# Rotary rows of two heads' queries and keys gathered into one 128-partition tile, turned there in four passes, and brought back

## The chip, the cores and the metric

The kernel runs on one core of a Trainium2 chip. The core has a matrix engine (TensorE, PE in the profile; PEld is its weight load), a vector engine (VectorE, DVE), a scalar engine (ScalarE, ACT), a general engine (GpSimd, POOL) and a synchronisation engine (SyncE, SP). Each takes its instructions in order from its own queue. Transfers are carried by 16 DMA engines and are issued here from SP, ACT and POOL. SBUF is the working memory with 128 partitions, PSUM holds the matmul accumulators, DRAM holds inputs, outputs and scratch. The metric is the device time of one execution in microseconds.

## The reference

A model of two layers for one sequence of 512 tokens of width 1024: an attention layer with three dilations, an mLSTM layer, and a gated feed-forward layer after each. Weights and activations are float32. The change lies in the attention layer, which for each of three groups projects queries, keys and values for eight heads of width 128, turns the first 32 of the 128 features of each query and key by the token's position, and attends within a window:

```python
def apply_partial_rope(t, positions):            # ROT_DIM = 32
    half = ROT_DIM // 2
    inv_freq = ROPE_THETA ** (-jnp.arange(half) * 2.0 / ROT_DIM)
    ang = positions[..., None] * inv_freq
    x1, x2 = t[..., :half], t[..., half:ROT_DIM]
    return concatenate([x1 * cos - x2 * sin, x2 * cos + x1 * sin, t[..., ROT_DIM:]])

def dilated_attention_mixer(xn, positions, w_in, w_out):
    proj = (xn @ w_in).reshape(B, S, N_GROUPS, 3, ATTN_HEADS, ATTN_HEAD_DIM)
    for g, (window, dilation) in enumerate(((128, 1), (512, 4), (2048, 16))):
        q = apply_partial_rope(proj[:, :, g, 0], positions) * scale
        k = apply_partial_rope(proj[:, :, g, 1], positions)
        o, lse = dilated_window_attention(q, k, proj[:, :, g, 2], window, dilation)
        ...
    wts = softmax(stack(lses))          # over the three groups
    return (sum over g of wts * o) @ w_out
```

## The kernel before

Activations lie with features on partitions and the 512 tokens along the free side. Every float32 product is made of three matmuls in a reduced float32 format, from high and low parts of weights and activations: ScalarE makes the high part of a weight chunk (line 208) and VectorE the low part (line 209), from a 512 KB load issued by SP (line 200). Three buffers each hold raw, high and low chunks, so the parts of a chunk are made about two chunks before TensorE uses them.

The attention layer works through four pairs of heads (`attention_pair`). For a pair it projects, for each of the groups 0, 1 and 2, the queries and then the keys of both heads (`project`, two chunks of 24 matmuls each, two accumulators of 128 features by 512 tokens). Then come the values of group 0 (two chunks) and the values of groups 1 and 2 together (`project_tokens_wide`, four chunks). The profile's names begin with the pair: a1g0q is the query projection of group 0 in pair 1.

An accumulator is left through `evac`: VectorE multiplies it by `rbc`, the inverse root mean square of each token, into a 128x2x512 tile (lines 730 and 732; group 0 changes the order of the tokens on the way). The first 32 partitions of the tile are the rotary rows. Before the change they are turned in three steps: `rope_part` shuffles the accumulator's 32 rows so that each row's partner is in its place (line 535), `rotate` multiplies both heads' shuffled rows by a table of scaled sines (line 538) and adds them (lines 541 and 543). The cosines are already in rows 0 to 31 of `rbc`, put there by `rope_scale` (lines 529 and 530) with the scaling of the token. All these instructions use 32 partitions.

What follows a projection is issued in *runs*, deferred by a counter of *ticks*: `advance` adds a tick after each chunk of a projection and calls what has come due. A run keeps its matmuls together in TensorE's order, and the matmuls of later projections stand behind it (`run`, `fenced`). So on TensorE the place of a run is fixed by its tick. On the other engines the order is set by the framework, by when it expects inputs to be ready. The lists below give the ticks:

```python
RUN_AT = (2, 3, 5, 10)
LAST_AT = (2, 4)
```

The first entry counts from the end of group 0's keys, the other three from the end of group 2's keys. They are:

- `scores0`, the scores of group 0 (matmuls at line 575), their maxima and exponentials;
- `scores12`, the scores of groups 1 and 2 (line 595), likewise;
- one run with `joint` (an exchange of maxima and sums between partitions, matmul at line 631, and the groups' weights), and for each head `weigh`, `transposes` (VectorE at line 687, then four writes to scratch in DRAM from POOL, line 690) and `bring` (one read of 960 KB from scratch, POOL, line 695, into a tile named pT);
- `values`, for each head the product of values and probabilities (lines 705 and 710), which reads pT.

In the last pair `LAST_AT` takes the place of the middle two, and the values are placed by hand among the chunks of the output projection.

POOL also carries, in each pair, the turn of group 0's values through scratch (eight writes of 64 KB at line 675, one read at line 677). Before the loops it copies the tables of sines and cosines into their place (lines 388 and 389).

Of the kernel before, what the change touches and what calls it, by code (L numbers as in the profile page):

```python
# [11 lines left out]
F32 = mybir.dt.float32  # L12
F32R = mybir.dt.float32r
I32 = mybir.dt.int32
AF = mybir.ActivationFunctionType
ALU = mybir.AluOpType
AX = mybir.AxisListType
P = 128

SEQ = 512  # L20
# [11 lines left out]
C1 = 6.28125  # L32
C2 = float(np.float32(np.uint32(np.float32(TWO_PI - C1).view(np.uint32) & 0xFFFFF000).view(np.float32)))
C3 = float(np.float32(TWO_PI - C1 - C2))
RUN_AT = (2, 3, 5, 10)
LAST_AT = (2, 4)
STACK_AT = (9, 11, 15, 17)
HEAD_AT = ((9, 10, 12, 14), (10, 11, 13, 15), (12, 13, 15, 17), (13, 14, 16, 18), (15, 16, 18, 19), (16, 17, 19, 21),
           (18, 19, 21, 22), (19, 20, 21, 23))
# [31 lines left out]
def tile_hybrid_dilated_attn_mlstm(  # L71
# [4 lines left out]
    nc = tc.nc  # L76
    x = x[0]
# [61 lines left out]
    def defer(n, fn):  # L139
        later.append((tick[0] + n, next(order), fn))  # L140
# [166 lines left out]
    def inverse_rms(v, name, box=None, then=None):  # L307

        r = npl.tile([P, TB], F32, tag="rtok", name=name + "r", bufs=2)
        rbc = npl.tile([P, SEQ], F32, tag="rbc", name=name + "rbc")  # L310
        parts = {}

        def finish():
            nc.vector.tensor_scalar(v, v, 1.0 / D, EPS, op0=ALU.mult, op1=ALU.add)
            rsqrt_newton(npl, v, TB, name + "r", r)
            rhl = npl.tile([P, 2, TB], F32R, tag="rhl", name=name + "rhl", bufs=2)
            nc.vector.tensor_copy(rhl[:, 0], r)
            nc.vector.tensor_tensor(rhl[:, 1], r, rhl[:, 0].bitcast(F32), op=ALU.subtract)
            for part in range(2):
                dg = parts[part] = npl.tile([P, SEQ], F32R, tag=("ssum", "sq")[part], name=name + "dg",  # L320
                                               bufs=1 + part)
                for tb in range(TB):
                    nc.vector.tensor_scalar(dg[:, tb * P:(tb + 1) * P], ident,
                                            rhl[:, part, tb:tb + 1].bitcast(F32), None, op0=ALU.mult)

        def hook():
            bp = ps.tile([P, 512], F32, tag="t", name=name + "bc", bufs=1)
            for part in range(2):
                nc.tensor.matmul(bp, ones_r, parts[part], start=(part == 0), stop=(part == 1))
            nc.vector.tensor_copy(rbc, bp)  # L330
            if then is not None:
                then(bp)
        if box is None:
            finish()
        else:
            box["finish"] = finish
        return rbc, r, hook
# [7 lines left out]
    with ExitStack() as actx:  # L345
        ap = pool(actx, "attn")
        dp = pool(actx, "scratch", space=bass.MemoryType.DRAM)

        R = 32
# [1 line left out]
        acst = ap.tile([P, K_END - K_MA], F32, name="acst")  # L351
        part = lambda at, w: acst[:, at - K_MA:at - K_MA + w]
        mask_band, mask_causal, mask_dil, perm = part(K_MA, 2 * P), part(K_M1, P), part(K_M2, P), part(K_G, P)
        cosn, sinn = (ap.tile([R, SEQ], F32, tag="pt", name=nm, bufs=2) for nm in ("cosn", "sinn"))
        sinr = ap.tile([R, SEQ], F32, name="sinr")

        posi = ap.tile([P, SEQ], I32, tag="rt", name="posi", bufs=2)
        nc.scalar.dma_start(posi.rearrange("(c r) s -> c r s", c=4)[:, 0], positions[0:1].to_broadcast([4, SEQ]))
        warm = cp.tile([P, 1], F32, name="warm")
        nc.scalar.activation(warm, ones[:, 0:1], AF.Sin)  # L360
# [19 lines left out]
        def rope_tables():  # L380
            nc.scalar.activation(sn, ang, AF.Sin)
            nc.scalar.activation(cs, ang, AF.Sin, scale=0.5)
            nc.vector.tensor_scalar(sn, sn, cst[:, K_SGN:K_SGN + 1], None, op0=ALU.mult)
            nc.vector.scalar_tensor_tensor(cs, cs, -2.0, cs, op0=ALU.mult, op1=ALU.mult)
            nc.vector.tensor_scalar(cs, cs, 1.0, None, op0=ALU.add)
            for c in range(4):
                s = slice(32 * c, 32 * c + 32)
                nc.gpsimd.tensor_copy(sinn[:, c * P:(c + 1) * P], sn[s])
                nc.gpsimd.tensor_copy(cosn[:, c * P:(c + 1) * P], cs[s])

        def tok_tile(name):
            return ap.tile([P, 2, SEQ], F32, tag="qk", name=name, bufs=6)
# [103 lines left out]
        nc.vector.tensor_tensor(v, ss2[:, 0], ss2[:, 1], op=ALU.add)  # L496
        behind(first_mm, 3)
        box = {}
        rbc, rtok, bc_hook = inverse_rms(v, "x", box, then=lambda bp: rope_scale(bp))
        behind(box["finish"], engine=DVE)  # L500
        both(lambda: ready.append(split_chunk(weight_chunk(w_in, 0, 3 * D, 4, "a0g1q_k0"))))
        for k in range(4, 8):
# [13 lines left out]
        defer(4, natural_rstd)  # L516
        defer(5, transpose_rows)

        def by_block(t):

            return t.rearrange("p (c b j) -> p b c j", c=4, b=TB)

        def in_order(t):
            return t.rearrange("p (b c j) -> p b c j", c=4, b=TB)

        def rope_scale(bp):
            nc.vector.tensor_tensor(sinr, bp[:R], sinn, op=ALU.mult)
            nc.vector.tensor_tensor(rbc[:R], bp[:R], cosn, op=ALU.mult)  # L530

        shift = [(k + 16) % 32 for k in range(32)]

        def rope_part(sh, m, acc):
            nc.vector.stream_shuffle(sh[:, m, :], acc[:R], shift)

        def rotate(t, sh, blocks):
            nc.vector.tensor_tensor(sh, sh, sinr.unsqueeze(1).to_broadcast([R, 2, SEQ]), op=ALU.mult)
            if blocks:
                for i in range(2):  # L540
                    nc.vector.tensor_tensor(in_order(t[:R, i]), in_order(t[:R, i]), by_block(sh[:, i]), op=ALU.add)
            else:
                nc.vector.tensor_tensor(t[:R], t[:R], sh, op=ALU.add)

        o_all = []

# [5 lines left out]
        def attention_pair(pr):  # L552
            nm = "a%d" % pr
# [165 lines left out]
            for g in range(3):  # L719
                base = g * 3 * D + pr * 256  # L720
                qk = []
                qks.append(qk)
                for part in range(2):
                    t = tok_tile("%sg%d_%s" % (nm, g, "qk"[part]))

                    sh = ap.tile([R, 2, SEQ], F32, tag="rt", name="rot", bufs=2)

                    def evac(m, acc, t=t, sh=sh, g=g):
                        if g == 0:
                            nc.vector.tensor_tensor(in_order(t[:, m]), by_block(acc), by_block(rbc), op=ALU.mult)  # L730
                        else:
                            nc.vector.tensor_tensor(t[:, m], acc, rbc, op=ALU.mult)
                        rope_part(sh, m, acc)
                    start = pr == 0 and g == 0 and part == 0
                    if start:
                        def first_evac(evac=evac):
                            bc_hook()
                            for m in range(2):
                                evac(m, facc[m])
                        defer(1, first_evac)  # L740
                    else:
                        project(pair, w_in, base + part * D, KC, evac, "%sg%d%s" % (nm, g, "qk"[part]), ready=ready)
                        if pr == 0 and g == 0:
                            rotate(qk[0], sh0, True)
                    if pr == 0 and g == 0 and part == 0:
                        sh0 = sh
                    else:
                        rotate(t, sh, g == 0)
                    qk.append(t)
                if g == 0:  # L750
                    defer(RUN_AT[0], lambda: run(lambda: scores0(*qks[0])))
            later_runs = (
# [376 lines left out]
    with ExitStack() as mctx:  # L1129
# [136 lines left out]
        i = 0  # L1266
# [275 lines left out]
```

## Time and profile before

| What | us |
|---|---|
| median of three runs | 1428.96 (1428.83 to 1429.31) |
| profiled execution | 1428.88 |
| its span | 1427.1 |
| TensorE busy in the span | 1415.9 |
| VectorE busy | 960.4 |
| ScalarE busy | 603.4 |
| POOL busy | 84.8 |

The attention layer takes about the first third of the span. A line of the timeline gives the start and the length in microseconds, the engine, the line of the kernel, the operation, what it writes and reads, the tile's shape and how many instructions are merged; in square brackets stand the idle time before it and what ended it. A matmul's length is modelled and overlaps the next one's, so the distance of two starts tells more than the length. A DMA line gives the bytes of one issue and the time from issue to landing. For a group of instructions three numbers with slashes are shortest, median and longest, in ns.

### The profile page before, as it was taken

How to read it: one execution, taken by the hardware profiler on the slowest of the kernel's cores; microseconds unless marked ns; L12 is line 12 of the kernel's file. 1: busy time of each engine (PE TensorE's matmuls, PEld its weight loads, DVE VectorE, ACT ScalarE, POOL GpSimd, SP SyncE). 2: the span in 40 equal slices, each digit the busy share in tenths (PEclk: the TensorE clock that was granted, in tenths of full speed). 3: DMA queues.
4: the chain of work that ended last, by engine and by line, in shares of the span. 5: the costliest groups of instructions: out<-in, count | busy, mean ns of one | idle time of the engine just before them, and what ended most of it. 6: DMA issues, size and time to landing. Idle time of an engine off the chain costs nothing. (4 is left out here: it accounts for less than half of the span.)

```text
span 1427.1 us, 20255 instructions
## 1 busy us (share of the span) xinstructions
PE 1415.9 (99%) x7986; PEld 1241.2 (87%) x7986; DVE 960.4 (67%) x1679; ACT 603.4 (42%) x1009; POOL 84.8 (6%) x137
## 2 busy tenths in 40 slices
PE   9999999999999999999999999999999999999998
PEld 7888888888888888999998888888888899998887
DVE  7857567567567397787782358897758777888233
ACT  5333224224225353444462233696534354445123
POOL 1011011011002000000000010110000000001001
PEclk9999999999999999999999999999999999999999
DMA  6346236235335434323233232321133332346331
GB/s 193 102 115 201 75 104 191 97 108 151 133 104 145 145 101 133 107 72 118 90 96 96 96 98 74 104 60 60 55 113 96 122 118 83 96 118 180 116 106 72
DMA packets 133688, 158.67 MB, mean 111 GB/s; under 512 B 7060, under 2 KB 121044, under 8 KB 133592
## 3 DMA queue, kind: packets, MB, share of 16 engines
q1 hardware_dynamic: 125616, 131.55, 29.6%
q0 software_dynamic: 6320, 24.69, 6.2%
q8 instruction: 63, 1.03, 0.3%
q10 hardware_dynamic: 1656, 1.12, 0.2%
q14 instruction: 33, 0.27, 0.1%
HBM read 143.18 MB, written 14.16 MB: 110 GB/s over the span
## 5 line engine op out<-in xcount | busy, mean ns | idle before, releaser
L1471 PE MATMUL fin<-fw_l,f1hh 128*128 128x512 f32 (+1 forms) x198 | 72.5, 366 | 0.0
L1471 PE MATMUL fin<-fw_h,f1hh 128*128 128x512 f32 (+1 forms) x198 | 72.4, 366 | 0.0
L1471 PE MATMUL fin<-fw_h,f1hl 128*128 128x512 f32 (+1 forms) x198 | 72.4, 365 | 0.0
L209 DVE TENSOR_TENSOR fo_k_l<-fo_k_w,fo_k_h 128x1024 fp32r<-128x1024 f32 (+1 forms) x24 | 27.2, 1135 | 62.0 <-ACT fo_k_h L208 62.0
L239 PE MATMUL fo<-f0hh,fo_k_h 128*128 128x512 f32 x176 | 68.5, 389 | 0.0
L239 PE MATMUL fo<-f0hl,fo_k_h 128*128 128x512 f32 x176 | 68.5, 389 | 0.0
L239 PE MATMUL fo<-f0hh,fo_k_l 128*128 128x512 f32 x176 | 68.5, 389 | 0.0
L209 DVE TENSOR_TENSOR fw_l<-fw_w,fw_h 128x1024 fp32r<-128x1024 f32 x22 | 27.1, 1233 | 59.9 <-ACT fw_h L208 59.9
L208 ACT ACTIVATE fo_k_h<-fo_k_w 128x1024 fp32r<-128x1024 f32 (+1 forms) x24 | 23.7, 989 | 74.7 <-PE fo L239 74.7
L208 ACT ACTIVATE fw_h<-fw_w 128x1024 fp32r<-128x1024 f32 x22 | 23.3, 1060 | 67.6 <-PE fin L1471 67.0
L1471 PEld LDWEIGHTS fin<-fw_l,f1hh 128*128 128x128 f32 x198 | 37.4, 189 | 6.2 <-DVE fw_l L209 0.2
L1471 PEld LDWEIGHTS fin<-fw_h,f1hh 128*128 128x128 f32 x198 | 37.3, 189 | 6.2
L1471 PEld LDWEIGHTS fin<-fw_h,f1hl 128*128 128x128 f32 x198 | 37.3, 188 | 6.0
L239 PEld LDWEIGHTS fo<-f0hh,fo_k_l 128*128 128x128 f32 x176 | 33.0, 188 | 6.9
L239 PEld LDWEIGHTS fo<-f0hl,fo_k_h 128*128 128x128 f32 x176 | 33.0, 188 | 6.9
L239 PEld LDWEIGHTS fo<-f0hh,fo_k_h 128*128 128x128 f32 x176 | 33.0, 188 | 6.7
L239 PE MATMUL f0j<-n_h,f0j_h 128*128 128x512 f32 x96 | 37.5, 390 | 0.0
L239 PE MATMUL f1j<-n_h,f1j_h 128*128 128x512 f32 x96 | 37.5, 390 | 0.0
L239 PE MATMUL f0j<-n_h,f0j_l 128*128 128x512 f32 x96 | 37.4, 389 | 0.0
L239 PE MATMUL f1j<-n_h,f1j_l 128*128 128x512 f32 x96 | 37.4, 389 | 0.0
L239 PE MATMUL f0j<-n_l,f0j_h 128*128 128x512 f32 x96 | 37.3, 389 | 0.0
L239 PE MATMUL f1j<-n_l,f1j_h 128*128 128x512 f32 x96 | 37.3, 389 | 0.0
(2105 smaller groups left out, 4886.0 us busy)
## 6 DMA issues: line engine op xcount, KB each, us to landing
f0j_w<-in_ffn_w_in_dram SPq DMA_DIRECT2D x28, 512.0 KB, 4.9
f1j_w<-in_ffn_w_in_dram SPq DMA_DIRECT2D x28, 512.0 KB, 4.4
fw_w<-in_ffn_w_out_dram SPq DMA_DIRECT2D x22, 512.0 KB, 3.9
fo_k_w<-in_ffn_w_out_dram SPq DMA_DIRECT2D x20, 512.0 KB, 3.5
awo_k_w<-in_attn_w_out_dram SPq DMA_DIRECT2D x8, 512.0 KB, 7.1
mv_k_w<-in_mlstm_w_in_dram SPq DMA_DIRECT2D x8, 512.0 KB, 3.7
mqk_k_w<-in_mlstm_w_in_dram SPq DMA_DIRECT2D x8, 512.0 KB, 3.9
mo_k_w<-in_mlstm_w_in_dram SPq DMA_DIRECT2D x8, 512.0 KB, 3.7
```

The lines of the kernel that those rows point to most:

```text
L208: nc.scalar.activation(hi[:, :n], raw[:, :n], AF.Copy)
L209: nc.vector.tensor_tensor(lo[:, :n], raw[:, :n], hi[:, :n].bitcast(F32), op=ALU.subtract)
L239: nc.tensor.matmul(acc, whl[a][:, k, m * P:(m + 1) * P], pairs[b][kk], start=(kk == 0 and (a, b) == SPLITS[0]), stop=(kk == nk - 1 and (a, ...
L1471: nc.tensor.matmul(acc[i][:, cs], a[a_][kk][:, tb * P:(tb + 1) * P], whl[b_][:, k, cs], start=(kk == 0 and (a_, b_) == SPLITS[0]), stop=(k ...
```

## The change

The rotary rows of a group, which are the first 32 partitions of both heads of the query tile and of the key tile, are gathered by four DMAs from POOL (`rope_gather`, `rope_rows`) into a tile `rt` of 128 partitions and 512 tokens. One tick after the keys of the group, `rotate` shuffles `rt` into a second tile, multiplies that by the sines and `rt` by the cosines, adds the two, and brings the four strips of 32 rows back by four more DMAs from POOL. The tables `cos4` and `sin4` are held four times over, on 128 partitions; six DMAs from POOL copy the first 32 rows to the others at the start. The tokens' scale now reaches the rotary rows through `evac` as it does the other rows, so the hook that scaled the tables is gone. The tiles of this work take four buffers of 2 KB a partition instead of two of 4 KB. The runs' ticks become (3, 4, 6, 10) and (3, 5).

```diff
--- before.py
+++ after.py
@@ -32,8 +32,8 @@
 C1 = 6.28125
 C2 = float(np.float32(np.uint32(np.float32(TWO_PI - C1).view(np.uint32) & 0xFFFFF000).view(np.float32)))
 C3 = float(np.float32(TWO_PI - C1 - C2))
-RUN_AT = (2, 3, 5, 10)
-LAST_AT = (2, 4)
+RUN_AT = (3, 4, 6, 10)
+LAST_AT = (3, 5)
 STACK_AT = (9, 11, 15, 17)
 HEAD_AT = ((9, 10, 12, 14), (10, 11, 13, 15), (12, 13, 15, 17), (13, 14, 16, 18), (15, 16, 18, 19), (16, 17, 19, 21),
            (18, 19, 21, 22), (19, 20, 21, 23))
@@ -351,10 +351,9 @@
         acst = ap.tile([P, K_END - K_MA], F32, name="acst")
         part = lambda at, w: acst[:, at - K_MA:at - K_MA + w]
         mask_band, mask_causal, mask_dil, perm = part(K_MA, 2 * P), part(K_M1, P), part(K_M2, P), part(K_G, P)
-        cosn, sinn = (ap.tile([R, SEQ], F32, tag="pt", name=nm, bufs=2) for nm in ("cosn", "sinn"))
-        sinr = ap.tile([R, SEQ], F32, name="sinr")
-
-        posi = ap.tile([P, SEQ], I32, tag="rt", name="posi", bufs=2)
+        cos4, sin4 = (ap.tile([P, SEQ], F32, name=nm) for nm in ("cos4", "sin4"))
+
+        posi = ap.tile([P, SEQ], I32, tag="rt", name="posi", bufs=4)
         nc.scalar.dma_start(posi.rearrange("(c r) s -> c r s", c=4)[:, 0], positions[0:1].to_broadcast([4, SEQ]))
         warm = cp.tile([P, 1], F32, name="warm")
         nc.scalar.activation(warm, ones[:, 0:1], AF.Sin)
@@ -385,8 +384,12 @@
             nc.vector.tensor_scalar(cs, cs, 1.0, None, op0=ALU.add)
             for c in range(4):
                 s = slice(32 * c, 32 * c + 32)
-                nc.gpsimd.tensor_copy(sinn[:, c * P:(c + 1) * P], sn[s])
-                nc.gpsimd.tensor_copy(cosn[:, c * P:(c + 1) * P], cs[s])
+                nc.gpsimd.tensor_copy(sin4[:R, c * P:(c + 1) * P], sn[s])
+                nc.gpsimd.tensor_copy(cos4[:R, c * P:(c + 1) * P], cs[s])
+
+            for t in (sin4, cos4):
+                for c in range(1, 4):
+                    nc.gpsimd.dma_start(t[32 * c:32 * c + 32], t[:R])
 
         def tok_tile(name):
             return ap.tile([P, 2, SEQ], F32, tag="qk", name=name, bufs=6)
@@ -496,7 +499,7 @@
         nc.vector.tensor_tensor(v, ss2[:, 0], ss2[:, 1], op=ALU.add)
         behind(first_mm, 3)
         box = {}
-        rbc, rtok, bc_hook = inverse_rms(v, "x", box, then=lambda bp: rope_scale(bp))
+        rbc, rtok, bc_hook = inverse_rms(v, "x", box)
         behind(box["finish"], engine=DVE)
         both(lambda: ready.append(split_chunk(weight_chunk(w_in, 0, 3 * D, 4, "a0g1q_k0"))))
         for k in range(4, 8):
@@ -516,8 +519,6 @@
         defer(4, natural_rstd)
         defer(5, transpose_rows)
 
-
-
         def by_block(t):
 
             return t.rearrange("p (c b j) -> p b c j", c=4, b=TB)
@@ -525,22 +526,30 @@
         def in_order(t):
             return t.rearrange("p (b c j) -> p b c j", c=4, b=TB)
 
-        def rope_scale(bp):
-            nc.vector.tensor_tensor(sinr, bp[:R], sinn, op=ALU.mult)
-            nc.vector.tensor_tensor(rbc[:R], bp[:R], cosn, op=ALU.mult)
-
         shift = [(k + 16) % 32 for k in range(32)]
 
-        def rope_part(sh, m, acc):
-            nc.vector.stream_shuffle(sh[:, m, :], acc[:R], shift)
-
-        def rotate(t, sh, blocks):
-            nc.vector.tensor_tensor(sh, sh, sinr.unsqueeze(1).to_broadcast([R, 2, SEQ]), op=ALU.mult)
-            if blocks:
-                for i in range(2):
-                    nc.vector.tensor_tensor(in_order(t[:R, i]), in_order(t[:R, i]), by_block(sh[:, i]), op=ALU.add)
-            else:
-                nc.vector.tensor_tensor(t[:R], t[:R], sh, op=ALU.add)
+        def rope_rows(rt, part, m):
+            i = 2 * part + m
+            return rt[R * i:R * (i + 1)]
+
+        def rope_gather(rt, t, part):
+
+            for m in range(2):
+                nc.gpsimd.dma_start(rope_rows(rt, part, m), t[:R, m])
+
+        def rotate(rt, qk, blocks):
+
+            sh = ap.tile([P, SEQ], F32, tag="rt", name="rot", bufs=4)
+            nc.vector.stream_shuffle(sh, rt, shift)
+            for x, table in ((sh, sin4), (rt, cos4)):
+                if blocks:
+                    nc.vector.tensor_tensor(in_order(x), in_order(x), by_block(table), op=ALU.mult)
+                else:
+                    nc.vector.tensor_tensor(x, x, table, op=ALU.mult)
+            nc.vector.tensor_tensor(rt, rt, sh, op=ALU.add)
+            for part, t in enumerate(qk):
+                for m in range(2):
+                    nc.gpsimd.dma_start(t[:R, m], rope_rows(rt, part, m))
 
         o_all = []
 
@@ -720,33 +729,27 @@
                 base = g * 3 * D + pr * 256
                 qk = []
                 qks.append(qk)
+                rt = ap.tile([P, SEQ], F32, tag="rt", name="%sg%drt" % (nm, g), bufs=4)
                 for part in range(2):
                     t = tok_tile("%sg%d_%s" % (nm, g, "qk"[part]))
 
-                    sh = ap.tile([R, 2, SEQ], F32, tag="rt", name="rot", bufs=2)
-
-                    def evac(m, acc, t=t, sh=sh, g=g):
+                    def evac(m, acc, t=t, g=g):
                         if g == 0:
                             nc.vector.tensor_tensor(in_order(t[:, m]), by_block(acc), by_block(rbc), op=ALU.mult)
                         else:
                             nc.vector.tensor_tensor(t[:, m], acc, rbc, op=ALU.mult)
-                        rope_part(sh, m, acc)
-                    start = pr == 0 and g == 0 and part == 0
-                    if start:
-                        def first_evac(evac=evac):
+                    if pr == 0 and g == 0 and part == 0:
+                        def first_evac(evac=evac, rt=rt, t=t):
                             bc_hook()
                             for m in range(2):
                                 evac(m, facc[m])
+                            rope_gather(rt, t, 0)
                         defer(1, first_evac)
                     else:
                         project(pair, w_in, base + part * D, KC, evac, "%sg%d%s" % (nm, g, "qk"[part]), ready=ready)
-                        if pr == 0 and g == 0:
-                            rotate(qk[0], sh0, True)
-                    if pr == 0 and g == 0 and part == 0:
-                        sh0 = sh
-                    else:
-                        rotate(t, sh, g == 0)
+                        rope_gather(rt, t, part)
                     qk.append(t)
+                defer(1, lambda rt=rt, qk=qk, g=g: rotate(rt, qk, g == 0))
                 if g == 0:
                     defer(RUN_AT[0], lambda: run(lambda: scores0(*qks[0])))
             later_runs = (
```

## The prediction

> **What bounds the kernel now.** I read the page first: the span, the engine shares and the chain that ended last; then the time by stretches of the attention stage, then TensorE's own waits.
>
> ```profile
> span 1427.1 us, 20255 instructions
> PE 1415.9 (99%) x7986; PEld 1241.2 (87%) x7986; DVE 960.4 (67%) x1679; ACT 603.4 (42%) x1009; POOL 84.8 (6%) x137
> ...
> PE 34%; DVE 3%; ACT 2%; issue 0%; ACTq 0%; DVEq 0%
> ...
> 0.00:50.00 50.00, 47.61 (x215) 38.27 (x216) 41.14 (x110) 24.27 (x44) 5.79 (x18) 1.00 0.50 158
> ...
> 100.00:150.00 50.00, 50.00 (x263) 42.89 (x262) 33.64 (x93) 19.28 (x50) 6.28 (x11) 1.00 0.56 174
> ...
> 450.00:500.00 50.00, 50.00 (x252) 42.50 (x251) 24.39 (x33) 16.05 (x23) 5.50 (x10) 1.00 0.51 158
> ...
> PE m1yT L305 <- ACT vaug L1169: 1.7, 1, 1.7
> PE idle L107 <- DVE idle_w L102: 1.5, 1, 1.5
> PE a0g0q L449 <- ACT first_h L439: 0.5, 1, 0.5
> PE m1nb L1312 <- ACT m0e L1322: 0.4, 1, 0.4
> PE xbc L329 <- DVE xdg L323: 0.3, 1, 0.3
> ```
>
> In the stretches the columns are length, PE, PEld, DVE, ACT and POOL busy, TensorE's granted clock, DMA share and GB/s. TensorE bounds the stage: it is busy throughout from 50 to 500 us, at full clock, and its waits for other engines come to 4.4 us in the whole program, none of them on the rotary work. VectorE, whose work the change removes, is busy 34 of 50 us. So what it saves buys time only where TensorE waits for it; what it delays costs time where a buffer now comes just in time. I looked for that second kind next: where work of the runs reaches TensorE.
>
> ```profile
> 98.43 3.73 PE L595 MATMUL a0s<-a0g_k,a0g_q 128*128 128x128 f32 x32
> ...
> 112.92 0.38 PE L631 MATMUL a0xps<-a0ex,acst 128*128 128x128 f32 x2
> ...
> 140.39 1.73 PE L705 MATMUL a0o<-a0pT,a0v 128*128 128x128 f32 x14
> ...
> 143.74 1.73 PE L705 MATMUL a0o<-a0pT,a0v 128*128 128x128 f32 x14
> ...
> 255.32 1.73 PE L705 MATMUL a1o<-a1pT,a1v 128*128 128x128 f32 x14
> ...
> 366.90 1.73 PE L705 MATMUL a2o<-a2pT,a2v 128*128 128x128 f32 x14
> ...
> 478.53 1.73 PE L705 MATMUL a3o<-a3pT,a3v 128*128 128x128 f32 x14
> 13.22 1.26 POOL L389 COPY cosn<-angles 32x128 f32<-32x128 f32 x4
> ...
> 128.97 0.56 POOL L695 DMA_DIRECT2D a0pT<-a0pD  x1
> 136.38 0.55 POOL L695 DMA_DIRECT2D a0pT<-a0pD  x1 [6.86 <-DMA a0pD<-a0pB]
> ...
> 247.35 0.55 POOL L695 DMA_DIRECT2D a1pT<-a1pD  x1 [6.36 <-DMA a1pD<-a1pB]
> ...
> 359.23 0.55 POOL L695 DMA_DIRECT2D a2pT<-a2pD  x1 [6.66 <-DMA a2pD<-a2pB]
> ...
> 465.73 0.55 POOL L695 DMA_DIRECT2D a3pT<-a3pD  x1 [6.58 <-DMA a3pD<-a3pB]
> a0pT<-a0pD POOLq DMA_DIRECT2D x1, 960.0 KB, 9.3
> a0pT<-a0pD POOLq DMA_DIRECT2D x1, 960.0 KB, 6.7
> ...
> a1pT<-a1pD POOLq DMA_DIRECT2D x1, 960.0 KB, 5.6
> ...
> a2pT<-a2pD POOLq DMA_DIRECT2D x1, 960.0 KB, 6.9
> ...
> a3pT<-a3pD POOLq DMA_DIRECT2D x1, 960.0 KB, 8.8
> ```
>
> These are TensorE's timeline, POOL's timeline and the DMA view in the window of one issue (last number: us from issue to landing). In pair 0 the second head's probabilities are brought by the issue at 136.38 and land 6.7 later, at 143.08; their first matmul starts at 143.74. The margin is **0.66 us**. In pair 1: 247.35 + 5.6 = 252.95 against 255.32, margin 2.37. Pair 2: 359.23 + 6.9 = 366.13 against 366.90, margin 0.77. Pair 3: 465.73 + 8.8 = 474.53 against 478.53, margin 4.00. The first head's read in pair 0, 128.97 + 9.3 = 138.27 against 140.39, has 2.1. TensorE does not wait here today, but only just.
>
> **The change, part by part.**
>
> *A tick.* The deferred runs are counted in ticks, one for each chunk of a projection; a chunk is 24 matmuls. From the scores (98.43) to the exchange (112.92) lie two ticks and the scores' own run. Taking 3.6 for that run (its 3.73 less the overlap of its last matmul), a tick is (14.49 - 3.6) / 2 = **5.44 us**.
>
> *RUN_AT's third value, 5 to 6, its fourth kept at 10.* The run that holds the exchange, the weighing, the transpositions, the writes to scratch and the reads back moves one tick later. The run of the values stays on its tick. The chain between the two thus loses 5.44 us of room, and it had 0.66, 2.37 and 0.77 us to spare. The exchange's input isn't the limit: the scores move by the same tick. LAST_AT's second value, 4 to 5, does the same to pair 3, which had 4.00.
>
> *Does the chain itself get shorter?* This is VectorE in pair 0:
>
> ```profile
> 113.33 0.29 DVE L633 TENSOR_TENSOR a0ex<-a0xps,cst 128x128 f32<-128x128 f32 x1 [2.84 <-PE a0xps L631]
> ...
> 123.08 1.22 DVE L209 TENSOR_TENSOR a1g0k_k_l<-a1g0k_k_w,a1g0k_k_h 128x1024 fp32r<-128x1024 f32 x1
> 124.21 2.17 DVE L687 STREAM_TRANSPOSE a0pB<-a0p 128x1920 f32<-128x1920 f32 x1
> ...
> 127.41 0.68 DVE L730 TENSOR_TENSOR a1g_q<-a1g0q,xrbc 128x512 f32<-128x512 f32 x1
> L538 DVE TENSOR_TENSOR rot<-rot,sinr x24: 1197/1206/1208, 39.1 to 419.4; 32x1024 f32<-32x1024 f32 x24
> ...
> L535 DVE STREAM_SHUFFLE rot<-a1g0q x2: 719/722/724, 128.0 to 130.3; 32x512 f32<-32x512 f32 x2
> ```
>
> From 113.33 to the end of the second transposition, 126.38, there is no rotary instruction, so nothing that the change removes shortens the chain. Moved to 118.8 to 131.8, it meets the evacuations of the next pair's first block: 127.41, and a second from the same projection. Two at 0.61 of pace (0.68 less overlap) are 1.2 us. Its bounds are 0 (the transposition goes first) and 2.4 (one more weight split of 1.2, as the one at 123.08, falls in). I take 1.2 for pairs 0 to 2, since both evacuations come due inside the moved window, and 0 for pair 3, which has no next pair. The writes and reads by DMA keep their times of today; their bounds are the fastest and slowest row of the read, 5.6 and 9.3.
>
> *The rotation.* Removed in each of 12 group-and-pair blocks: four shuffles of 32x512 (L535, 0.72), two products of 32x1024 (L538, 1.21), and as much again in additions, which I price like the products. A pass over 512 elements takes 0.68 on 128 partitions (L730) and 0.72 on 32 (L535), so its price follows its length and not its partitions; I price each 128x512 pass at 0.7. A block goes from 4 x 0.7 + 4 x 1.2 = 7.6 us to 4 x 0.7 = 2.8, and VectorE loses some 58 us of 960. By the first fence this buys TensorE nothing: 0.
>
> *The gathers and returns.* Each block issues eight 64 KB transfers from POOL, 96 in all, and six more replicate the tables. No row has a copy from SBUF to SBUF; nearest is the 64 KB piece of the value turn, and the slowest read sets the other end:
>
> ```profile
> a0vD<-a0vB POOLq DMA_DIRECT2D x8, 64.0 KB, 3.0
> ...
> L675 POOL DMA_DIRECT2D a0vD<-a0vB x8: 648/648/692, 92.2 to 98.1; - x8
> 128.00:140.39 12.39, 12.39 (x56) 10.25 (x55) 8.16 (x14) 2.15 (x3) 1.97 (x4) 1.00 0.99 339
> ```
>
> Per block the new path is: two issues (1.3), landing (3.0), four passes (2.8), four issues (2.6), landing (3.0): 12.7 us after the last evacuation. For the scores of group 0 the run now stands three ticks after the block, 16.3 us, plus the values of two heads, 2 x 3.35 (143.74 - 140.39), in pairs 1 to 3; for groups 1 and 2 it stands four ticks after group 2, 21.8 us, and three, 16.3, in pair 3. Covered by 3.6 us in pair 0 and at pair 3's end and by 9 or more elsewhere: 0. If that cover goes, TensorE stands at the scores. With both landings at 9.3 the path is 25.3 us: 9.0 late in pair 0, 2.3 late three times for group 0, 3.5 late three times for groups 1 and 2, and 9.0 late at pair 3's end. That is the upper end, 36 us. I take 0, the row of equal size being the nearest; the other is of fifteen times the bytes.
>
> VectorE waits in order for the gather. Behind it queue weight splits, made two chunks (10.9 us) ahead, and the next evacuation of an accumulator (room about 5 us); a wait of 4.3 us (1.3 + 3.0) fits. POOL's queue: in pairs 0 to 2 the gathers stand about the read at 136.38, which waits for the writes. The next scores are far enough for that. The reverse, a gather's bytes ahead of the read in a stretch that moves 339 GB/s at a DMA share of 0.99, costs 128 KB / 339 = 0.4 us; it lies within the 9.3.
>
> *The head of the program.* The table copies on POOL end at 14.5 us (L389) and the six replications (6 x 0.65 + 3.0 = 6.9 us) at 21.4, while the first rotation is due after 39 (L538's first start). The two scalings of tables, gone with the hook, free VectorE after TensorE has got going. TensorE's waits there, 1.5, 0.5 and 0.3, are for other work: 0.
>
> *The waits themselves.* I count a wait at its length, with TensorE at full clock after it; the second rival prices the other case, up to 5.7 us more.
>
> **The sum.** Stall = 5.44 + 1.2 - margin: pair 0 5.98, pair 1 4.27, pair 2 5.87; pair 3 5.44 - 4.00 = 1.44. Together **17.6 us** on the profiled execution's 1428.88 (span 1427.1 and 1.8 around it): 1446.4. The median of the runs is 1428.96, 0.1 above it. About 0.2%, 2.9 us, is what a measurement of this kernel can tell from no change.
>
> **Rivals.**
> - *The tick is absorbed, no change.* The reads land early enough where they now stand, since the chain is mostly transfers and the crowd of 128 to 140 us need not move with it. It decides if the chain shortens by 4.7 us in pair 0. For it: reads vary from 5.6 to 9.3. Against: even 5.6 instead of 6.7 wins back 1.1. It gives 1428.9; the relief of VectorE adds at most the 0.3 us wait for xdg. A gain beyond 2.9 us has no wait to come from.
> - *The clock falls in the new waits.* TensorE would now stand idle at the values' start: in pair 0 until 128.97 + 6.64 + 9.3 = 144.91, 4.5 us.
>
> ```profile
> 1418.00:1422.00 4.00, 2.45 (x21) 2.25 (x19) 2.27 (x10) 1.90 (x7) 2.24 (x3) 1.00 0.35 135
> 1422.00:1427.00 5.00, 0.00 (x0) 0.00 (x0) 1.00 (x4) 0.72 (x1) 0.26 (x1) 0.61 0.27 105
> ```
>
> At the end of the program the granted clock drops to 0.61 in the first five idle microseconds. If a stall does that, the first head's 3.35 us of matmuls (143.74 - 140.39) could double; the second head waits 1.5 anyway, so 1.9 us more in each of three pairs: 1452. Against it: 4 to 4.5 us idle is little more than the drop needs. The Trainium skill's page "TensorE: Matmul & The Clock Gate", section "What's actually happening", says the gate halves the clock after an idle window of about 3.4 us, the window running freely. By that rule not every stall would be hit; the last rows agree that idleness lowers the clock, and no run here shows how long it takes.
> - *The rotary path is late too*, by the slow landings above: up to 1446 + 36 = 1482; 1.0 of landing more on each side still costs nothing, and 2.0 begins to.
>
> **How the numbers follow.** Forecast with the clock kept 0.70; clock falls 0.10; rotary path late 0.07; absorbed 0.13, of which 0.03 for a gain I have not seen. Low end of the forecast: no added VectorE work and reads at 5.6 give 3.7 + 3.1 + 3.4 + 0 = 10.2, or 1439. High end: 2.4 added and reads at 9.3 give 9.8 + 9.2 + 9.5 + 1.9 = 30.4, or 1459. The range 1436 to 1459 holds these and the clock's 1452; outside stay the absorbed case and most of the late one, 0.2. Faster 0.03, same 0.10, slower 0.87.
>
> **What would show it.** Right: TensorE waits at L705 for the DMA of the probabilities, some 4 to 6 us in pairs 0 to 2 and 1 to 2 in pair 3, and nowhere else in the stage; the exchange stands 5.4 us later; VectorE's busy time is near 902. Wrong: waits at L575 or L595 for a return (late rotary path), at L239 for a split or an evacuation (VectorE blocked behind a gather), a granted clock under 1.00 after 140 us, or no wait at L705.

## The result, and the profile after

| | before | changed |
|---|---|---|
| median, us | 1428.89 (1428.82 to 1429.31) | 1451.03 (1448.16 to 1453.39) |
| profiled execution, us | 1428.88 | 1448.16 |
| its span, us | 1427.1 | 1446.4 |
| VectorE busy, us | 960.4 | 907.5 |

The changed kernel takes 1.0153 times as long as the kernel before (95% interval 1.0134 to 1.0173): 22 us more by the medians, 19.3 by the two profiled executions. VectorE does 53 us less.

The page of the changed kernel, its span and engines:

```profile
span 1446.4 us, 20355 instructions
PE 1423.8 (98%) x7986; PEld 1247.5 (86%) x7986; DVE 907.5 (63%) x1585; ACT 602.1 (42%) x1009; POOL 135.7 (9%) x239
```

TensorE's waits in the changed kernel (total us, times, longest). Behind the inserted lines the values' matmuls stand at L714 and L719, the writes to scratch at L699 and the reads at L704:

```profile
PE a2o L714 <- DMA a2pT<-a2pD: 3.2, 1, 3.2
PE a1o L714 <- DMA a1pT<-a1pD: 3.1, 2, 2.6
PE a0o L714 <- DMA a0pT<-a0pD: 2.8, 2, 2.4
PE a3o L714 <- DMA a3pT<-a3pD: 1.8, 1, 1.8
PE m1yT L305 <- ACT vaug L1172: 1.7, 1, 1.7
```

The first four rows are new; the fifth was there before. All four are waits for the probabilities, in the values, one row per pair. No row names a score (L584, L604) or a projection (L239): TensorE doesn't wait for the rotary work.

The waits come to 10.9 us, but the loss is larger. How late a pair's work comes is read best from the first matmul of two projections, one ahead of the values of the pair before (a1g0k, a2g0k, a3g0k, and for the last pair the output projection awo) and one behind them (a1g1q, a2g1q, a3g1q, and f0j of the next layer):

| values of | start ahead, before and changed | start behind, before and changed | lost between |
|---|---|---|---|
| pair 0 | 129.51, 129.76 | 147.01, 152.14 | 4.9 |
| pair 1 | 241.09, 246.24 | 258.59, 269.02 | 5.3 |
| pair 2 | 352.67, 363.13 | 370.17, 386.74 | 6.1 |
| pair 3 | 453.37, 469.96 | 503.69, 522.31 | 2.0 |

These sum to 18.3 of the 19.3 us; the rest lies ahead of pair 0's values (0.25), between the rows (0.07) and after the attention layer (0.7). TensorE's and POOL's timelines in pair 0 of the changed kernel (start, length), and the second read in the DMA view of its issue:

```profile
118.61 0.38 PE L640 MATMUL a0xps<-a0ex,acst 128*128 128x128 f32 x2
...
143.22 2.56 PE L714 MATMUL a0o<-a0pT,a0v 128*128 128x128 f32 x14 [2.42 <-DMA a0pT<-a0pD]
145.57 2.87 PE L719 MATMUL a0o<-a0pT,a0v 128*128 128x128 f32 x16
148.77 1.83 PE L714 MATMUL a0o<-a0pT,a0v 128*128 128x128 f32 x14 [0.34 <-DMA a0pT<-a0pD]
...
131.81 2.18 POOL L699 DMA_DIRECT2D a0pD<-a0pB  x4 [2.28 <-DVE a0pB L696]
133.98 0.56 POOL L704 DMA_DIRECT2D a0pT<-a0pD  x1
...
140.97 0.55 POOL L704 DMA_DIRECT2D a0pT<-a0pD  x1 [6.44 <-DMA a0pD<-a0pB]
...
a0pT<-a0pD POOLq DMA_DIRECT2D x1, 960.0 KB, 7.8
```

The exchange stands at 118.61 in place of 112.92, the second read at 140.97 in place of 136.38, and lands 7.8 later, at 148.8. The second head's matmuls start on that moment. From the exchange to that landing are 30.2 us, as many as before (143.08 - 112.92); only the room was cut.

The first head's matmuls are spread out, too: 5.55 us from 143.22 to 148.77, of which 0.34 is a wait, where 3.35 was the pace. The stretches of the changed kernel (length, PE, PEld, DVE, ACT and POOL busy, granted clock, DMA share, GB/s) say why:

```profile
143.00:144.00 1.00, 0.78 (x7) 0.81 (x8) 0.00 (x0) 0.00 (x0) 0.51 (x2) 1.00 1.16 356
144.00:145.00 1.00, 1.00 (x8) 1.00 (x7) 0.00 (x0) 0.00 (x0) 0.00 (x0) 0.53 1.03 350
145.00:146.00 1.00, 1.00 (x7) 1.00 (x7) 0.00 (x0) 0.00 (x0) 0.00 (x0) 0.50 0.98 397
146.00:147.00 1.00, 1.00 (x6) 1.00 (x6) 0.00 (x0) 0.00 (x0) 0.00 (x0) 0.50 1.06 381
147.00:148.00 1.00, 1.00 (x9) 1.00 (x8) 0.00 (x0) 0.00 (x0) 0.00 (x0) 0.76 0.96 248
```

After the wait the granted clock is halved for some 3.4 us, until 147.5. Those who read only the waits' lengths see 2.8 us in pair 0 and miss that the first head's slow matmuls hide most of what would have been a second wait. In pair 2 they do more than hide it: the second head's read lands at 382.78 and its matmuls start at 383.47.

### The profile page after: what moved, and what is told of

It is laid out like the page before. It is cut to its first block, busy times and chain, and to the rows that moved or that the text cites. A ratio compares the mean times of both kernels' runs of the same rounds, so it can differ in the third digit from the quotient of the medians.

```text
span 1446.4 us, 20355 instructions
## 1 busy us (share of the span) xinstructions
PE 1423.8 (98%) x7986; PEld 1247.5 (86%) x7986; DVE 907.5 (63%) x1585; ACT 602.1 (42%) x1009; POOL 135.7 (9%) x239
## 5 line engine op out<-in xcount | busy, mean ns | idle before, releaser
L239 PE MATMUL fo<-f0hl,fo_k_h 128*128 128x512 f32 x176 | 68.5, 389 | 0.0
L239 PE MATMUL fo<-f0hh,fo_k_h 128*128 128x512 f32 x176 | 68.5, 389 | 0.0
L239 PE MATMUL fo<-f0hh,fo_k_l 128*128 128x512 f32 x176 | 68.5, 389 | 0.0
L239 PEld LDWEIGHTS fo<-f0hh,fo_k_l 128*128 128x128 f32 x176 | 33.0, 188 | 6.9
L239 PEld LDWEIGHTS fo<-f0hl,fo_k_h 128*128 128x128 f32 x176 | 33.0, 188 | 6.9
L239 PEld LDWEIGHTS fo<-f0hh,fo_k_h 128*128 128x128 f32 x176 | 33.0, 188 | 6.7
L239 PE MATMUL f0j<-n_h,f0j_h 128*128 128x512 f32 x96 | 37.5, 390 | 0.0
L239 PE MATMUL f1j<-n_h,f1j_h 128*128 128x512 f32 x96 | 37.5, 390 | 0.0
L239 PE MATMUL f1j<-n_h,f1j_l 128*128 128x512 f32 x96 | 37.4, 389 | 0.0
L239 PE MATMUL f0j<-n_h,f0j_l 128*128 128x512 f32 x96 | 37.4, 389 | 0.0
L239 PE MATMUL f0j<-n_l,f0j_h 128*128 128x512 f32 x96 | 37.4, 389 | 0.0
L239 PE MATMUL f1j<-n_l,f1j_h 128*128 128x512 f32 x96 | 37.4, 389 | 0.0
```

Of the source, the lines that this page charges most:

```text
L239: nc.tensor.matmul(acc, whl[a][:, k, m * P:(m + 1) * P], pairs[b][kk], start=(kk == 0 and (a, b) == SPLITS[0]), stop=(kk == nk - 1 and (a, ...
```

## The experiments

Theory: the third due time, which moves exchange, writes and reads one tick towards the values, is the cause, and the rotary work by DMA costs nothing. Rivals: the rotary path (gathers, returns, waits for them), or the fallen clock.

### The due times alone, and the rotary work alone

e1 is the kernel before with the later ticks for all runs but the first:

```diff
-RUN_AT = (2, 3, 5, 10)
-LAST_AT = (2, 4)
+RUN_AT = (2, 4, 6, 10)
+LAST_AT = (3, 5)
```

> The kernel before with its old rotary work, and only the ticks moved: the scores of groups 1 and 2 at 4 and the exchange's run at 6 instead of 3 and 5, in the last pair 3 and 5 instead of 2 and 4; the scores of group 0 stay at 2. Theory (the moved exchange run eats the room between it and the values): about 1429 + 18 = 1447, from 1445 to 1453, with waits at the values' matmuls for the reads of the probabilities of 2 to 4 us in each of pairs 0 to 2, and a granted clock of 0.5 for some microseconds after them. Rival (the rotary transfers and POOL's longer queue make the loss): within 2 us of 1429, no such wait.

e2 is the changed kernel with the old ticks for all runs but the first:

```diff
-RUN_AT = (3, 4, 6, 10)
-LAST_AT = (3, 5)
+RUN_AT = (3, 3, 5, 10)
+LAST_AT = (2, 4)
```

> The changed kernel with the ticks of the scores of groups 1 and 2 and of the exchange's run put back to 3 and 5, in the last pair 2 and 4; only the scores of group 0 stay at 3. Theory (ticks): the waits at the values go, 1429 to 1431; the rotary path of some 11 us is covered by the 16.3 us of three ticks. Rival (the rotary transfers lengthen the reads by themselves): a loss stays, 1434 to 1445, with waits at the values or at the scores.

Measured: e1 1444.23 us, ratio 1.0099 (1.0082 to 1.0116); e2 1430.41 us, ratio 1.0008 (0.9999 to 1.0017). The new rotary work without the two later ticks costs nothing that can be told from 0.2%; the ticks without the new rotary work cost 15 us, 0.8 less than e1's range allowed. In e2 TensorE has no wait for the probabilities. Its first and second head in pair 0 start one behind the other:

```profile
140.63 1.73 PE L714 MATMUL a0o<-a0pT,a0v 128*128 128x128 f32 x14
...
144.25 1.83 PE L714 MATMUL a0o<-a0pT,a0v 128*128 128x128 f32 x14
```

But the medians left something open. Against the kernel before in the same executions (1429.21) the ticks alone cost 15.0 us and the rotary work alone 1.2; both together cost 22.1. That is some 6 us more than the sum.

### Which of the due times

e3 gives the room back at the other end, with the values one tick later:

```diff
-RUN_AT = (3, 4, 6, 10)
+RUN_AT = (3, 4, 6, 11)
```

> The changed kernel with the values one tick later too, 11 for 10; the last pair as in the change. Theory (room between the exchange and the values): pairs 0 to 2 get back 5.4 us and wait no more, pair 3 keeps its 2 us: 1431, from 1429.5 to 1433, with a granted clock of 1.00 to 480 us. Rival (transfers late by more than a tick, or the later values delay the next scores): 1436 or more.

e9 puts back the third due time alone, e10 leaves it alone as changed:

```diff
-RUN_AT = (3, 4, 6, 10)
-LAST_AT = (3, 5)
+RUN_AT = (3, 4, 5, 10)
+LAST_AT = (3, 4)
```

> The changed kernel with the third due time alone put back (6 to 5, and 5 to 4 in the last pair); first and second stay at 3 and 4. Theory (the third due time, which starts the exchange of the maxima and with it writes and reads of the probabilities, is the whole cause): 1430 to 1433 us; up to 1 us more if the exchange, one tick behind the two other scores instead of two, has to wait for them. Rival (the later scores themselves hold up the chain): 1440 us or more.

```diff
-RUN_AT = (3, 4, 6, 10)
-LAST_AT = (3, 5)
+RUN_AT = (3, 3, 6, 10)
+LAST_AT = (2, 5)
```

> The changed kernel with first and second due time at 3 and 3 (2 in the last pair), and the third alone as in the change, 6 (5 in the last pair). Theory (the third due time is the whole cause): waits for the probabilities as in the changed kernel, 1446 to 1453 us. Rival (it takes the second too): under 1440 us.

Measured: e3 1432.56 us, ratio 1.0026 (1.0017 to 1.0036); e10 1451.64 us, ratio 1.0151 (1.0136 to 1.0166); e9 1436.96 us, ratio 1.0055 (1.0038 to 1.0071). e10 has the change's whole loss, though it differs from e2 in one number of each list alone, and e3 takes all but 3.4 us of it away by giving the chain its tick back; what e3 has left includes waits of 0.7 and 1.8 us for the probabilities in pairs 2 and 3, and none was expected in pair 2. e9 lies 4 us above its range, 3 with the 1 us that it allowed for a wait of the exchange, and the waits of its TensorE tell where:

```profile
PE a3xps L640 <- DVE a3ex L635: 1.7, 1, 1.7
...
PE a0xps L640 <- DVE a0ex L635: 1.2, 1, 1.2
PE a2xps L640 <- DVE a2ex L635: 1.2, 1, 1.2
PE a1xps L640 <- DVE a1ex L635: 1.1, 1, 1.1
...
PE a0o L714 <- DMA a0pT<-a0pD: 0.2, 1, 0.2
```

The waits for the probabilities are gone but for 0.2, as the theory says. In their place TensorE waits at the exchange, 5.2 us in all: one tick behind the other scores VectorE hasn't their maxima ready. So the exchange is hemmed in from both sides, two ticks behind the scores and five ahead of the values.

### What the rotary path costs

e5 is the changed kernel with all the old ticks, so that the first scores come two ticks after the keys; e6 has them after one:

```diff
-RUN_AT = (3, 4, 6, 10)
-LAST_AT = (3, 5)
+RUN_AT = (2, 3, 5, 10)
+LAST_AT = (2, 4)
```

> The changed kernel with all four due times of the kernel before (2, 3, 5, 10 and 2, 4): the rotary path by DMA gets 10.9 us instead of 16.3 us before the first scores. Theory (the rotary path costs some 11 us after the last evacuation, by the changed kernel's trace 36.6 to about 46.5 to 48.5 us in pair 0): a wait of 0 to 2 us on TensorE at the first scores of pair 0, none in pairs 1 to 3, time 1429.5 to 1433 us. Rival (the later due times of the change were needed): waits of several us in each pair, 1440 us or more.

```diff
-RUN_AT = (2, 3, 5, 10)
+RUN_AT = (1, 3, 5, 10)
```

> As e5, but the first scores one tick after the keys: 5.44 us of cover in place of 10.9 us. This prices the rotary path: with scores due at 41.2 us in pair 0 and the last return landing at 46.5 to 48.5 us, TensorE waits 5 to 7 us there, and 0 to 3 us in each of pairs 1 to 3, whose returns land at about 155 us (pair 1) against scores due at 153 us. Time 1436 to 1444 us. Were the path shorter than the trace lets it look, under 1433 us.

Measured: e5 1430.94 us, ratio 1.0014 (1.0005 to 1.0024); e6 1438.67 us, ratio 1.0070 (1.0055 to 1.0085). VectorE's last evacuation of the keys in pair 0, POOL's last gather and last returns, and the first scores on TensorE, all of e5:

```profile
47.02 3.27 PE L584 MATMUL a0s<-a0g_k,a0g_q 128*128 128x128 f32 x16 [1.27 <-DMA a0g_k<-a0g0rt]
...
34.78 0.69 DVE L738 TENSOR_TENSOR a0g_k<-a0g0k,xrbc 128x512 f32<-128x512 f32 x1 [0.48 <-PE a0g0k L239]
...
38.66 0.73 DVE L543 STREAM_SHUFFLE rot<-a0g0rt 128x512 f32<-128x512 f32 x1
...
35.76 0.50 POOL L538 DMA_DIRECT2D a0g0rt<-a0g_k  x1 [0.68 <-DVE a0g_k L738]
...
42.80 1.00 POOL L552 DMA_DIRECT2D a0g_k<-a0g0rt  x2
```

From the end of the last evacuation, 35.47, to the scores at 47.02 are 11.6 us. The two ticks, 10.9 us, count from the end of the keys' matmuls at 34.58 and are over at 45.46, which, behind two small matmuls, leaves the 1.27 us wait. In e6, with one tick, the same row waits 5.88 us, and then 1.5 us more go to a halved clock (the scores' 3.27 us become 4.72). In pairs 1 to 3 neither has a wait there, the low end of the 0 to 3 us that e6 expected in each: of the 8.2 us between the two profiled executions 7.6 are lost before pair 1's keys of group 0 begin (130.4 against 138.0). So the first due time does need a tick more for the new path, but only in pair 0 and for 1.3 us.

### The clock

e4 is the changed kernel with 14 matmuls of 128x512, whose result nobody reads, ahead of the values of pairs 0 to 2; e8 is e1 with 11 of them:

```diff
+            def fill():
+                fp_ = ps.tile([P, 512], F32, tag="t", name=nm + "fill", bufs=1)
+                for k in range(14):
+                    nc.tensor.matmul(fp_, ones_r, pair[0][0], start=True, stop=True)
...
-                later_runs += ((lambda: values(0), lambda: values(1)),)
+                later_runs += ((fill, lambda: values(0), lambda: values(1)),)
```

> The changed kernel with 14 extra matmuls of 128x512 into an unused bank ahead of the values in pairs 0 to 2, 14 x 0.226 = 3.2 us of work whose result nobody reads, in the place of the wait. Theory A (the reads set the time, the clock's fall is hidden behind the second head's read): the same as the change in its fastest run, 1447 to 1449. Theory B (the fallen clock adds its own time and makes the spread from 1448 to 1453): 1443 to 1447 with a spread under 1 us, clock 1.00 in the values, and the second head's matmuls starting when its read lands. If the fill is longer than the wait, up to 1 us a pair comes on top.

> The kernel before with the due times of e1, and 11 matmuls of 128x512 whose result nobody reads ahead of the values of pairs 0 to 2, so that TensorE doesn't stand idle there. Theory (in e1 the second head's probabilities are there at 146.4 us, but the first head's products run at half clock, 5.05 us in place of 3.4 us, so the second starts only at 148.5): the second head's values start at about 146.8, 263.0 and 378.8 us, 1.5 us sooner per pair, 1439 to 1442 us. Rival (the fallen clock costs nothing beside the reads): 1444 us as e1.

Measured: e4 1449.82 us (1447.17 to 1453.79), ratio 1.0145 (1.0127 to 1.0164), against 1.0153 of the change; e8 1440.31 us, ratio 1.0083 (1.0068 to 1.0098), against 1.0099 of e1. The median of e4 is 0.8 above theory A's range and further from theory B's. In e4's profile, of its shortest execution, the clock stays up, the first head is done in time, and TensorE then waits 1.9 us for the second head in pairs 0 and 1. It is 1.0 us shorter than the change's profile (1447.17 against 1448.16): as far as two single profiles tell, the fallen clock cost the change about that much. The spread is not gone, 6.6 us, and in e4's three longer executions the mean granted clock is 0.997, 0.997 and 0.995 against 0.999, so there the filling did not keep it up. In e8 it is otherwise. The values of e1 in pair 0, the stretch behind their wait, and the same place in e8 (whose inserted lines make L705 L710):

```profile
143.45 3.03 PE L705 MATMUL a0o<-a0pT,a0v 128*128 128x128 f32 x14 [2.54 <-DMA a0pT<-a0pD]
146.27 2.40 PE L710 MATMUL a0o<-a0pT,a0v 128*128 128x128 f32 x16
148.50 1.73 PE L705 MATMUL a0o<-a0pT,a0v 128*128 128x128 f32 x14
...
144.00:145.00 1.00, 1.00 (x7) 1.00 (x7) 0.00 (x0) 0.00 (x0) 0.00 (x0) 0.50 1.01 407
```

```profile
143.17 1.72 PE L710 MATMUL a0o<-a0pT,a0v 128*128 128x128 f32 x14
...
146.60 1.83 PE L710 MATMUL a0o<-a0pT,a0v 128*128 128x128 f32 x14
```

In e1 the second head needn't wait for its read, only for the slow first head; with the clock kept up it starts 1.9 us sooner, at 146.60. In pairs 1 and 2 it starts at 261.88 and 376.76, and the projections behind the values of pairs 0, 1 and 2 (a1g1q, a2g1q, a3g1q) stand 1.8, 2.8 and 3.3 us sooner than in e1, so pair 0 brings the most and the others 1.0 and 0.5. By the medians e8 is 3.9 us faster; the profiles differ by more, 5.7 us, but e1's is of its longest execution, and 2.5 of it lie in pair 3, which isn't filled and where e1's clock fell as well. The fallen clock costs where the second head's read lands early, and is mostly hidden where it lands late.

### Why both together cost more

The read of the second head is issued as soon as its four writes have landed. In e1 that is 2.4 us sooner than in the changed kernel, though the writes begin at the same time. This is SP's timeline of the changed kernel and the DMA view of the last writes of the second head (issued between 133.0 and 133.8), ahead of them VectorE's split that frees the raw buffer (a group of one instruction, with its duration in ns and its start):

```profile
L209 DVE TENSOR_TENSOR a1g0k_k_l<-a1g0k_k_w,a1g0k_k_h x1: 1203/1203/1203, 132.0 to 132.0; 128x1024 fp32r<-128x1024 f32 x1
...
133.25 1.50 SPq L200 DMA_DIRECT2D a1g1k_k_w<-in_attn_w_in_dram  x2
...
a0pD<-a0pB POOLq DMA_DIRECT2D x2, 240.0 KB, 6.4
```

In the changed kernel the split ends at 133.2, and SP, which has waited for that buffer, issues the next weight load at 133.25, while POOL still issues the writes that began at 131.81. In e1 the old shuffles hold VectorE up, the load goes out at 134.61, behind all four writes, and they land in 4.5 us at most. e7 tests this: the changed kernel, with the two old shuffles per projection of group 0 put back, to no use.

```diff
-                    def evac(m, acc, t=t, g=g):
+                    def evac(m, acc, t=t, g=g, rt=rt, part=part):
                         if g == 0:
                             nc.vector.tensor_tensor(in_order(t[:, m]), by_block(acc), by_block(rbc), op=ALU.mult)
+                            nc.vector.stream_shuffle(rope_rows(rt, part, m), acc[:R], shift)
```

> The changed kernel with the two shuffles of 0.7 us per projection of group 0 put back on VectorE (their result is overwritten by the gathers and used by nothing). Theory (in the changed kernel VectorE splits the raw weights sooner, so SP issues the next weight load at 133.2 us in place of 134.6 us and its bytes run beside the second head's writes of probabilities, which land up to 2.5 us later): the load goes back to 134.5 us or so, the second head's read is issued at 138.5 to 139.5 us instead of 141.0, and the time falls to 1443 to 1447 us though VectorE does more. Rival (the gathers' own bytes or POOL's issues hold up the reads): the second read stays at 141 us, 1449 to 1452 us.

Measured: 1443.60 us (1440.81 to 1444.89), ratio 1.0101 (1.0086 to 1.0116). VectorE does 11.5 us more than in the changed kernel (919.0), and the kernel is 7.4 us faster. By the profiles it stands 1.6, 3.5 and 6.6 us ahead of the changed kernel behind the values of pairs 0, 1 and 2. Its clock stays up there, so some 1 us of this may be the clock's. The same rows in e7, with POOL's timeline and TensorE's wait in pair 0:

```profile
L209 DVE TENSOR_TENSOR a1g0k_k_l<-a1g0k_k_w,a1g0k_k_h x1: 1226/1226/1226, 133.2 to 133.2; 128x1024 fp32r<-128x1024 f32 x1
...
134.47 2.12 SPq L200 DMA_DIRECT2D a1g1k_k_w<-in_attn_w_in_dram  x2
...
131.52 2.18 POOL L699 DMA_DIRECT2D a0pD<-a0pB  x4 [2.28 <-DVE a0pB L696]
...
138.37 0.55 POOL L704 DMA_DIRECT2D a0pT<-a0pD  x1 [4.13 <-DMA a0pD<-a0pB]
...
a0pD<-a0pB POOLq DMA_DIRECT2D x2, 240.0 KB, 4.5
...
PE a0o L714 <- DMA a0pT<-a0pD: 3.0, 2, 1.6
```

In pair 0, counted from the start of the second head's writes:

| kernel | weight load issued | second read issued |
|---|---|---|
| before | +0.84 | +9.70 |
| e2 | +0.84 | +8.96 |
| changed | +1.44 | +9.16 |
| e1 | +2.72 | +6.67 |
| e8 | +2.71 | +6.92 |
| e7 | +2.95 | +6.85 |

The load ahead of the last write goes with a late read, the load behind it with an early one, in old and new rotary work alike. In pairs 1 and 2 the changed kernel has +1.44 with +9.41 and +9.46, and e1 +2.71 and +2.70 with +6.76 and +6.74. All twelve profiles and all four pairs agree: in 39 cases a load is issued at +0.84 to +1.44, and the second read follows at +8.7 to +10.0; in the other 9 (pairs 0 to 2 of e1, e7 and e8) no load comes before +2.70, and the read follows at +6.7 to +7.2. The gathers aren't it: e7 has them all. The DMA view of the 4 us from 3 to 7 us after the start of the second head's writes shows what the load takes (packets, MB, share of the 16 engines; q0 is POOL's queue, with these writes and the first head's read, q1 SP's), first in the changed kernel, then in e7:

```profile
DMA packets 616, 1.01 MB, mean 253 GB/s; under 512 B 48, under 2 KB 513, under 8 KB 616
q0 software_dynamic: 142, 0.53, 56.6%
q1 hardware_dynamic: 474, 0.48, 33.7%
```

```profile
DMA packets 224, 1.01 MB, mean 253 GB/s; under 512 B 48, under 2 KB 52, under 8 KB 224
q0 software_dynamic: 220, 1.01, 88.5%
q1 hardware_dynamic: 4, 0.00, 0.3%
```

Both move 1.01 MB; in the changed kernel nearly half of it is the weight load's. No run moves the load alone: e7 moves it by way of VectorE's work.

## Why the prediction was right, and where it was not

The forecast was 1446.4, the profiled execution took 1448.16 and the median is 1451.03, inside the range.

- *TensorE is the bound, what VectorE saves buys nothing.* Right: 53 us less on VectorE (58 forecast), and e2 stays at 1.0008.
- *The third due time takes a tick from the chain.* Right: with this tick alone the whole loss is there (e10), and with the tick given back most of it goes (e3). But some 6 us of that loss come only together with the lighter VectorE work (e1, e7). The exchange moved by 5.69 us against 5.44.
- *The second head's read has margins of 0.66, 2.37 and 0.77 us.* Right for pairs 0 to 2. In pair 3 the forecast took the same read with 4.00 us; what decided was the first head's: issued at 481.19 it landed 9.7 later, at 490.9, and the values started at 490.99.
- *1.2 us more on VectorE in the moved chain.* Wrong in sign. From the exchange's first VectorE instruction to the end of the second transposition it was 13.05 us (113.33 to 126.38) and is now 12.49 (119.03 to 131.52): one evacuation of 0.68 came in, and one of the two weight splits of 1.2 fell out.
- *Writes and reads keep their times.* The mis-sized term on the other side. The second reads took 7.8, 7.9 and 8.1 us in place of 6.7, 5.6 and 6.9. The two errors nearly cancel: stalls of 4.9, 5.3, 6.1 and 2.0 were forecast at 5.98, 4.27, 5.87 and 1.44, together 18.3 and 17.6. That the sums stand so close is in part luck.
- *Full clock after the waits.* Wrong: the clock fell in pairs 0 to 2, which is the second rival's mechanism and one of the forecast's own signs of being wrong. Its price of 1.9 us a pair did not come in the change, where the clock cost some 1.0 us in all by the profiles (e4); without the faster VectorE it came in pair 0 and in part in the others (e8). With the first head slowed, the longest waits at L714 were 2.4 to 3.2 us in pairs 0 to 2 and not 4 to 6. The forecast held that 4 to 4.5 us idle is little more than the drop needs, but its own two rows put the drop 2.7 us after the last matmul (1418 + 2.45 = 1420.45; a mean of 0.61 over 5 us is full clock for 1.1 us and half clock behind, so 1423.1), and a wait of 1.89 us was enough in e1.
- *The rotary path takes 12.7 us and is covered.* Right: 11.6 us in e5, and no wait in the change. Single terms differ: an issue takes 0.50 us and not 0.65, the last returns land after 4.0 us and not 3.0. (The upper end that the forecast gave for a late path is 36 us; its parts sum to 35.4.) In pairs 1 to 3 the gathers of group 0 stand on POOL behind the second read and land 7.2 to 8.6 us after their issue, so VectorE waits 7.5 to 8.2 us, where the forecast allowed 4.3; that too was harmless. The row of pair 1 in the changed kernel:

```profile
DVE rot L543 <- DMA a1g0rt<-a1g_k: 7.5, 1, 7.5
```

- *What the forecast did not see* is that a faster VectorE frees a raw weight buffer sooner, and that the load so released runs into the writes. It looked at VectorE's savings only for what they take from TensorE's waits. The 4.6 us between forecast and median are of that size (e7 is 7.4 below the change), but the parts can't be told apart: the change's own executions spread over 5.2 us, those of e10 over 4.4, and only the shortest of the change's has a profile here. The longer ones of the change have a lower mean clock (0.995, 0.995, 0.993 and 0.992 from the shortest to the longest); whether that lengthens them or comes of longer waits is not shown.

No version beat the kernel before. The best with the new rotary work, e2, is level with it; before and after, TensorE is busy 98 to 99% of the span.

## What to carry to other kernels

Before moving a run by a tick, subtract: list what the run starts and when its last transfer lands against the first use. A margin of 0.66 us can't pay a tick of 5.44. Work taken off an engine that isn't the bound still moves what that engine releases; look for the transfers that start sooner and for what they then share the DMA engines with.

## What was unexpected in the hardware

- The granted clock fell to 0.50 after waits of 1.89 (e1, pair 2), 2.42 (the change, pair 0) and 3.19 us (the change, pair 2), and stayed there for 3.4 us, in pair 2 of the change for 6.8. After waits of 1.82 (the change, pair 3), 1.89 (e4, pair 0) and 1.62 (e7, pair 0) it did not fall, so the wait's length alone doesn't decide. Where a wait lies does. These are more stretches of the changed kernel, with the columns of those in the section on the result:

```profile
260.00:261.00 1.00, 1.00 (x6) 1.00 (x7) 0.00 (x0) 0.00 (x0) 0.23 (x1) 0.56 1.12 337
263.00:264.00 1.00, 1.00 (x9) 1.00 (x8) 0.00 (x0) 0.00 (x0) 0.00 (x0) 0.74 1.06 329
376.00:377.00 1.00, 0.00 (x0) 0.00 (x0) 0.30 (x1) 0.00 (x0) 1.00 (x3) 0.58 1.11 364
```

  A mean of 0.56 over 1 us is full clock for 0.12 us and half clock behind, so the clock fell at 260.12; likewise it fell at 144.06 (0.53) and 376.16 (0.58), and rose at 147.48 (0.76) and 263.52 (0.74). It is down for one step of about 3.41 us, in pair 2 for two, and the falls are 116.06 and 116.04 us apart, 34 such steps each. Cut into steps on this grid (each profile's own falls, the one behind its last matmul included, say where the steps begin), the twelve profiles tell the cases apart: all 11 falls from 12 us on and before the last matmul came at the end of a step in which TensorE had been idle for 1.89 us or more, and no step with 1.82 us or less was followed by one. The 1.89 us of e4 lay across a border, 1.78 of them in one step. The Trainium skill's page "TensorE: Matmul & The Clock Gate", section "What's actually happening", has the gate close after an idle window of about 3.4 us that runs freely. The grid agrees with a free window of that length; a window that must be idle throughout does not, since 1.89 of 3.41 us were enough.
- Weight loads of 512 KB, the first issued 1.4 us after the first of four writes of 240 KB and so ahead of the last, went with a read behind those writes 2.4 us later than loads of which the first was issued 2.7 us after it (the change and e1, pair 0).
